# Where the weight buffers of a projection lie in the SBUF partition: moving them down, in a hybrid decoder block on one Trainium2 core

## The chip, the core and the metric

The kernel runs on one core of a Trainium2 chip. Its time is the device time of one execution, in microseconds; the time before is the median of three executions. Times inside the kernel come from one execution that the hardware profiler recorded.

## The reference, cut to what matters

All data is float32: 512 tokens, width 2048.

```python
h  = rms_norm(x, norm1_g);  z = h @ w_in                # 2048 -> 9216 columns in 72 tiles of 128
zs = token_shift(z[:, :3520], rw_mu)                    # r, k, v and three small inputs
o_rw  = rwkv7_mix(zs, ...)                              # 16 heads of 64, a recurrence over the tokens
o_att = swa_attention(q, k, v, ...)                     # 16 heads, window 128
p_rw, p_att = o_rw @ w_branch[:1024], o_att @ w_branch[1024:]
x = x + (sigmoid(zg_rw) * p_rw + sigmoid(zg_att) * p_att) @ w_out
x = x + conv_ffn(rms_norm(x, norm2_g), w_up, conv_w, conv_b, w_down)
```

## The kernel before

Every large product is made of float32r matmuls in threes: each operand is split into a high part (ACT, a copy) and a low part (DVE, a subtraction), and the products high·high, low·high and high·low are summed in PSUM. A matmul has a **stationary** operand (128 x 128, loaded by a LDWEIGHTS, engine PEld in the profile) and a **moving** one that streams past it.

The stages, in order of time:

- **Input projection with attention and RWKV inside it** (34.7 to 1240.3 us). `project` (L251) works on one tile of 128 columns: 16 steps over the width, each of three matmuls (L259 to L261) with 512 moving columns. Stationary are the weights `whi`, `wlo`; moving are the activations `xhi`, `xlo`. `load_w` (L237) brings weights in groups of four steps: SP issues the DMA into a buffer `raw` (L241), ACT writes `whi` (L244), DVE writes `wlo` (L245); every third group it also issues a step of the sums of the output weights (L228 on SP's queue, L229 on POOL's). There are 72 tiles, so 3456 such matmuls. The attention's and RWKV's small matmuls, which wait for ACT and DVE, stand between them; 32 gate tiles of the projection (`emit_gate`, L322) are kept back as filling, and the last of them stand behind RWKV. A scheduler orders the instructions; what is marked `pin` keeps the program's order.
- **Branch projection** (1240.3 to 1414.5 us): the same `project` and `load_w`, 768 matmuls; moving are `rhi`, `rlo` (RWKV's result) and `ahi`, `alo` (the attention's).
- **Output projection** (from 1414.5 us to about 1577): Strassen-like products in seven parts (`steps_of`, L944). Here the *left factors* `hhi`, `hlo` (from `fetch`, L937, which loads `hraw`) are stationary and the weights `whi`, `wlo` (pool hlD, L955 and L954) are moving, 512 columns (L962): 672 matmuls in threes with the stationary operands `hhi`, `hlo`, `hhi`.
- **Feed-forward up** (1577 to 2490 us): weights stationary, activations `b..`, `t..` moving with 256 columns (L1095). **Down** (2490 to 2914 us): `steps_of` again.

SBUF gives each of the 128 partitions one address range. Pools stand on it from two sides, "left" (growing up) and "right" (growing down). The places that the built programs give the operands of this study, in KiB from the start of the partition:

| operand | use | before | after the change |
|---|---|---|---|
| input projection `whi`, `wlo` | stationary | 204.0 to 216.0 (3 buffers each) | 97.8 to 113.8 (4 each) |
| its `raw` | DMA in | 216.0 to 224.0 | 89.8 to 97.8 |
| `xhi`, `xlo`; later `ahi`, `alo` | moving | 25.8 to 89.8 | the same |
| branch projection `whi`, `wlo` | stationary | 145.8 to 161.8 (4 each) | 97.8 to 113.8, the same buffers |
| `rhi`, `rlo` | moving | 89.8 to 121.8 | 113.8 to 145.8 |
| RWKV `BX`, `BV`, `BKK` | stationary | 105.9 to 117.9 | 129.9 to 141.9 |
| RWKV `AB`, `KK`, `SV`, `UV`, `AI`, `BT` | stationary | 125.9 to 129.9, 133.9 to 145.9, 147.9 to 155.9 | 141.9 to 165.9 |
| RWKV `BAR`, `MM` | moving | 117.9 to 125.9, 129.9 to 133.9 | 165.9 to 177.9 |
| RWKV `BKE` / `lg` (tag lw) / `lg`'s square / `gn` | stationary | 185 / 156 / 162 / 194 | 209 / 180 / 186 / 218 |
| attention `pr` | stationary | 157 to 165 | 181 to 189 |
| output projection `hhi` / `hlo` / `hraw` | stationary / stationary / DMA in | 178.7 to 184.7 / 184.7 to 190.7 / 172.7 to 178.7 | 172.7 to 178.7 / 178.7 to 184.7 / 184.7 to 190.7 |
| down `hhi`, `hlo` | stationary | 80.5 to 92.5 | 74.5 to 86.5 |
| weights of both Strassen stages and of up (`whi`, `wlo` of hlD) | moving / stationary in up | 18.5 to 42.5 | the same |
| `b11`, `b21`, `b22`, `t1`, `t3`, `t2`, `t4` | moving in up | 74.5 to 186.5 | the same |

## Time and profile before

| | |
|---|---|
| time, median of three executions | 2914.16 us (2914.02 to 2918.12) |
| span of the profiled execution, first to last instruction | 2913.7 us, 0.5 us below that median |
| PE busy | 98% of the span |
| chain that ended last | PE 94%, DVE 2%, ACT 1%, DMA 1% |
| granted TensorE clock | 0.997 over the span |

How to read it: a row of the costliest groups gives line, engine, operation, tiles (written<-read), shape and count, then busy time and the mean duration of one in ns. Matmuls are pipelined: a duration covers streaming and the way through the array, so one starts before the one ahead has ended, and durations of 390 ns stand for a start every 227 ns or so. The pace is therefore taken from counts in a stretch of time in which nothing but such matmuls run.

### The profile page before, as it was taken

Reading aid. Unit: us, or ns where it says so; the run is one execution under the profiler, and the core shown is the slowest. Engines: PE = TensorE matmul, PEld = TensorE weight load, DVE = VectorE, ACT = ScalarE, POOL = GpSimd, SP = SyncE. Lnnn points to the kernel's source line nnn. Section 1 sums busy time; section 2 is a strip of 40 time slices with the busy share of each in tenths; the row PEclk is TensorE's granted clock in tenths of the full one; section 3 lists DMA queues with packets and bytes.
Section 4 is the critical chain, followed back from the end, with each engine's and each line's share of the span. In section 5 each row is a group of like instructions: output and inputs, shape, how many; then the busy total and the mean of one; then the engine's idle time right before and its main releaser. Section 6 shows DMA issues by size and latency. Waiting matters only on the chain.

```text
span 2913.7 us, 46929 instructions
## 1 busy us (share of the span) xinstructions
PE 2868.1 (98%) x18014; PEld 2441.3 (84%) x18014; DVE 1970.2 (68%) x3383; ACT 1333.6 (46%) x2251; POOL 219.3 (8%) x286
## 2 busy tenths in 40 slices
PE   7999999999999999999999899999999999999999
PEld 5777777777777777788888899999999999888887
DVE  4577666667767766354567777787777777665565
ACT  4345435435435434322356455545555455544444
POOL 0001000000000000111000010111111100000000
PEclk9999999999999999999999999999999999999999
DMA  7856756656656655878877788988889888877775
GB/s 210 217 146 166 184 142 168 156 145 163 159 149 149 167 148 139 266 222 239 293 251 226 208 227 231 242 233 231 221 235 238 237 227 234 312 242 240 259 255 188
DMA packets 225137, 609.29 MB, mean 209 GB/s; under 512 B 24768, under 2 KB 44944, under 8 KB 223888
## 3 DMA queue, kind: packets, MB, share of 16 engines
q1 hardware_dynamic: 157504, 434.84, 45.9%
q0 software_dynamic: 36064, 132.14, 23.9%
q10 hardware_dynamic: 31344, 39.31, 4.0%
q8 instruction: 141, 2.31, 0.3%
q14 instruction: 84, 0.69, 0.1%
HBM read 556.54 MB, written 174.43 MB: 251 GB/s over the span
## 4 chain that ended last, share of the span: by engine, by line
PE 94%; DVE 2%; ACT 1%; DMA 1%; issue 0%; SPq 0%; DVEq 0%; ACTq 0%
PE X L1095 17%; PE acc L259 11%; PE X L962 11%; PE acc L261 11%; PE acc L260 11%; PE Y L1095 9%; PE Y L962 8%; PE Z L1095 4%; PE bulk L737 1%; PE bulk L690 1%; PE psG L744 1%; PE bulk L646 1%; PE psS L755 1%; PE mi L464 1%; PE scp L431 1%; PE bulk L554 1%
## 5 line engine op out<-in xcount | busy, mean ns | idle before, releaser
L259 PE MATMUL acc<-xhi,whi 128*128 128x512 f32 x1152 | 473.1, 411 | 5.0 <-ACT whi L244 3.1
L261 PE MATMUL acc<-xhi,wlo 128*128 128x512 f32 x1152 | 469.2, 408 | 0.0
L260 PE MATMUL acc<-xlo,whi 128*128 128x512 f32 x1152 | 467.1, 405 | 0.0
L244 ACT ACTIVATE whi<-raw 128x512 fp32r<-128x512 f32 x352 | 220.3, 630 | 492.8 <-PE acc L260 376.6
L955 DVE TENSOR_TENSOR wlo<-raw,whi 128x1024 fp32r<-128x1024 f32 x210 | 257.0, 1224 | 204.9 <-ACT whi L954 203.4
L245 DVE TENSOR_TENSOR wlo<-raw,whi 128x512 fp32r<-128x512 f32 x352 | 240.2, 689 | 207.3 <-ACT whi L244 195.4
L954 ACT ACTIVATE whi<-raw 128x1024 fp32r<-128x1024 f32 x210 | 222.8, 1061 | 287.9 <-PE X L962 147.1
L1095 PE MATMUL X<-b,whi 128*128 128x256 f32 x1472 | 270.2, 284 | 2.2 <-DVE u L1115 0.9
L1095 PE MATMUL X<-t,whi 128*128 128x256 f32 x1408 | 260.2, 285 | 8.7 <-DVE u L1115 8.3
L1078 DVE TENSOR_TENSOR wlo<-raw,whi 128x1024 fp32r<-128x1024 f32 x176 | 215.0, 1222 | 77.4 <-ACT whi L1077 77.2
L259 PEld LDWEIGHTS acc<-xhi,whi 128*128 128x128 f32 x1152 | 217.5, 189 | 52.8 <-ACT whi L244 4.4
L261 PEld LDWEIGHTS acc<-xhi,wlo 128*128 128x128 f32 x1152 | 217.3, 189 | 48.2 <-issue 2.2
L1095 PE MATMUL Y<-t,whi 128*128 128x256 f32 x1408 | 257.5, 283 | 0.0
L260 PEld LDWEIGHTS acc<-xlo,whi 128*128 128x128 f32 x1152 | 217.7, 189 | 44.9 <-issue 3.3
L1077 ACT ACTIVATE whi<-a 128x1024 fp32r<-128x1024 f32 x132 | 139.4, 1056 | 213.8 <-DVE a L1071 211.2
L1095 PEld LDWEIGHTS X<-b,whi 128*128 128x128 f32 x1472 | 230.3, 193 | 3.0 <-issue 2.3
L1095 PEld LDWEIGHTS X<-t,whi 128*128 128x128 f32 x1408 | 222.0, 194 | 9.3 <-DVE u L1115 5.7
L1095 PEld LDWEIGHTS Y<-t,whi 128*128 128x128 f32 x1408 | 220.1, 192 | 0.0
L1095 PE MATMUL X<-b,wlo 128*128 128x256 f32 x736 | 208.9, 284 | 2.1 <-DVE wlo L1078 2.1
L1078 DVE TENSOR_TENSOR wlo<-a,whi 128x1024 fp32r<-128x1024 f32 x132 | 161.7, 1225 | 67.7 <-ACT whi L1077 67.0
L1095 PE MATMUL X<-t,wlo 128*128 128x256 f32 x704 | 200.5, 285 | 0.0
L1095 PE MATMUL Y<-t,wlo 128*128 128x256 f32 x704 | 199.3, 283 | 0.0
(345 smaller groups left out, 5877.7 us busy)
## 6 DMA issues: line engine op xcount, KB each, us to landing
raw<-in_w_up_dram SPq DMA_DIRECT2D x180, 512.0 KB
raw<-in_w_z_dram SPq DMA_DIRECT2D x288, 256.0 KB
s_dn<-in_w_dn_dram POOLq DMA_DIRECT2D x88, 512.0 KB, 6.7
raw<-in_w_up_dram POOLq DMA_DIRECT2D x88, 512.0 KB, 8.1
raw<-s_dn SPq DMA_DIRECT2D x88, 512.0 KB
raw<-in_w_dn_dram SPq DMA_DIRECT2D x66, 512.0 KB
a<-in_w_up_dram SPq DMA_DIRECT2D x48, 512.0 KB
s_dn<-in_w_dn_dram SPq DMA_DIRECT2D x44, 512.0 KB
```

What stands on the lines that cost most here:

```text
L244: act.activation(hi, raw, AF.Copy)
L245: dve.tensor_tensor(lo, raw, hi.bitcast(F32), op=ALU.subtract)
L259: pe.matmul(acc, whi[:, j], xhi[:, k], start=first, stop=False)
L260: pe.matmul(acc, whi[:, j], xlo[:, k], start=False, stop=False)
L261: pe.matmul(acc, wlo[:, j], xhi[:, k], start=False, stop=last)
L431: pe.matmul(scp[e][:, j, k0:], qn[j][hs, ts], kd[g][hs, n * P - BLK + k0 : (n + 1) * P], start=True, stop=True)
L954: act.activation(whi, wr, AF.Copy)
L955: dve.tensor_tensor(wlo, wr, whi.bitcast(F32), op=ALU.subtract)
L962: pe.matmul(dst, l[:, q, ts], r[:, es], start=fst and j == 0, stop=lst and j == 2, skip_group_check=True)
L1077: pin(act.activation(hi, t, AF.Copy))
L1078: pin(dve.tensor_tensor(lo, t, hi.bitcast(F32), op=ALU.subtract))
L1095: pin(pe.matmul(ps, l[:, k], r[:, k], start=start and k + i == 0, stop=last and i == 2, skip_group_check=True))
```

## The change

The pool of the weight buffers is opened once, at the kernel's start, on the left side next to `xhi` and `xlo`, with four buffers each for `raw`, `whi` and `wlo`, and both projections use it; before, each projection opened its own (the input projection 4, 3 and 3 on the right, the branch projection 4, 4 and 4 on the left). RWKV's tiles are declared in another order, the left operands of its matmuls first, and `fetch` declares `hhi`, `hlo` before `hraw`. No arithmetic and no DMA is added or taken away.

```diff
     big1 = abc.enter_context(tc.tile_pool(name="big1", bufs=1))
+    wp = {"n": 0, "step": 3}
+    for nm in ("raw", "hl"):
+        wp[nm] = abc.enter_context(tc.tile_pool(name="w" + nm, bufs=4, reuse_waits="tile"))
     xin = ExitStack()
...
-    def open_weights(stack, nraw, nhl, side):
-        wp["raw"] = stack.enter_context(tc.tile_pool(name="wraw", bufs=nraw, side=side, reuse_waits="tile"))
-        wp["hl"] = stack.enter_context(tc.tile_pool(name="whl", bufs=nhl, side=side, reuse_waits="tile"))
...
-    open_weights(pa, 4, 3, "right")
...
+            AB, KK, SV, UV = (bd.tile([P, NCH, 2, C], F32, name=n) for n in ("AB", "KK", "SV", "UV"))
+            AI = bd.tile([P, 2, NCH, P], F16, name="AI")
+            BT = bd.tile([P, 2, NCH, P], F16, name="BT")
...
             BAR = bd.tile([P, NCH, 2, 2, C], F32, name="BAR")
...
-            AB, MM, KK, SV, UV = (bd.tile([P, NCH, 2, C], F32, name=n) for n in ("AB", "MM", "KK", "SV", "UV"))
...
+            MM = bd.tile([P, NCH, 2, C], F32, name="MM")
             Et = bd.tile([P, NCH, C + 1], F32, name="Et")
             pool.memset(Et[:, :, 0:1], 1.0)
-            AI = bd.tile([P, 2, NCH, P], F16, name="AI")
-            BT = bd.tile([P, 2, NCH, P], F16, name="BT")
...
-        open_weights(pbb, 4, 4, "left")
...
+        hhi, hlo = (pl.tile([P, 2, TH], F32R, name=f"h{e}", tag=f"h{e}") for e in ("hi", "lo"))
         hr = pl.tile([P, 2, TH], F32, name="hraw", tag="hraw")
         pin(sync.dma_start(hr, right_d[w][c][RIGHT_AT[PRODUCTS[i][3]]]))
-        hhi, hlo = (pl.tile([P, 2, TH], F32R, name=f"h{e}", tag=f"h{e}") for e in ("hi", "lo"))
```

In the order of the built programs, PE's instructions from RWKV to the end stand as before; inside the attention some matmuls change places by a few positions, and the two score matmuls of the first block of a head group (L431) stand up to 56 projection matmuls later. On ACT and DVE a few of the splits L244 and L245 stand one place earlier or later. On SP's queue the loads of the branch projection's first weights, eight of which stood among the last loads of the input projection, now follow all of these, and the gate loads of the first tile (L891) stand before the last 17 loads of the input projection.

More of the change, by code (lines that the diff above doesn't have):

```diff
@@ L229, in sums_along @@
         return lambda: pool.dma_start(dst, quarter(w, second, c)[q], accum_op=ALU.add, max_dma_last_dim=4096)
-    wp = {"n": 0, "step": 3}
-    def open_weights(stack, nraw, nhl, side):
-        wp["raw"] = stack.enter_context(tc.tile_pool(name="wraw", bufs=nraw, side=side, reuse_waits="tile"))
-        wp["hl"] = stack.enter_context(tc.tile_pool(name="whl", bufs=nhl, side=side, reuse_waits="tile"))
     def load_w(src):
@@ L529, in block_kernel @@
             BKK = bd.tile([P, NCH, P], F32, name="BKK")
+            AB, KK, SV, UV = (bd.tile([P, NCH, 2, C], F32, name=n) for n in ("AB", "KK", "SV", "UV"))
+            AI = bd.tile([P, 2, NCH, P], F16, name="AI")
+            BT = bd.tile([P, 2, NCH, P], F16, name="BT")
+            pool.memset(SV[0:C, 0, 0], 0.0)
+            pool.memset(SV[C:P, 0, 1], 0.0)
             BAR = bd.tile([P, NCH, 2, 2, C], F32, name="BAR")
@@ L532, in block_kernel @@
             pool.memset(BAR[C:P, :, 0], 0.0)
-            AB, MM, KK, SV, UV = (bd.tile([P, NCH, 2, C], F32, name=n) for n in ("AB", "MM", "KK", "SV", "UV"))
-            pool.memset(SV[0:C, 0, 0], 0.0)
-            pool.memset(SV[C:P, 0, 1], 0.0)
+            MM = bd.tile([P, NCH, 2, C], F32, name="MM")
             Et = bd.tile([P, NCH, C + 1], F32, name="Et")
             pool.memset(Et[:, :, 0:1], 1.0)
-            AI = bd.tile([P, 2, NCH, P], F16, name="AI")
-            BT = bd.tile([P, 2, NCH, P], F16, name="BT")
             def r3(ap, c=C):
```

## The prediction

> **What bounds the kernel now.** I read the page first, then the waits of PE in the input projection, then one question the page can't answer: how fast a full-size matmul follows the next, stage by stage.

> ```profile
> PE 2868.1 (98%) x18014; PEld 2441.3 (84%) x18014; DVE 1970.2 (68%) x3383; ACT 1333.6 (46%) x2251; POOL 219.3 (8%) x286
> ...
> PE 94%; DVE 2%; ACT 1%; DMA 1%; issue 0%; SPq 0%; DVEq 0%; ACTq 0%
> ...
> L259 PE MATMUL acc<-xhi,whi 128*128 128x512 f32 x1152 | 473.1, 411 | 5.0 <-ACT whi L244 3.1
> L261 PE MATMUL acc<-xhi,wlo 128*128 128x512 f32 x1152 | 469.2, 408 | 0.0
> L260 PE MATMUL acc<-xlo,whi 128*128 128x512 f32 x1152 | 467.1, 405 | 0.0
> ```

> PE sets the end nearly everywhere, and in the input projection (3 x 1152 = 3456 matmuls of 512 columns) it hardly waits: 5.0 us before L259, none before L260 and L261. So only what shortens PE's own steps, or its few waits, counts.

> The next view is the table by stage, for stretches in which nothing but such matmuls run: two of the input projection (272 and 1220 us), the branch projection, the output projection, the down projection. Columns: stretch, length, busy time and count of each engine, granted clock, DMA share, GB/s.

> ```profile
> 272.00:314.00 42.00, 42.00 (x182) 34.09 (x181) 17.00 (x27) 14.26 (x23) 8.36 (x15) 1.00 0.79 215
> 1220.00:1239.00 19.00, 19.00 (x83) 15.43 (x82) 5.87 (x9) 5.67 (x10) 1.63 (x2) 1.00 0.89 242
> 1245.00:1405.00 160.00, 160.00 (x707) 132.54 (x706) 79.61 (x134) 40.34 (x66) 17.01 (x24) 1.00 0.83 253
> 1416.00:1555.00 139.00, 139.00 (x597) 111.84 (x596) 90.86 (x110) 72.34 (x98) 7.99 (x14) 1.00 0.78 259
> 2500.00:2900.00 400.00, 400.00 (x1767) 331.31 (x1766) 238.10 (x245) 193.95 (x220) 0.00 (x0) 1.00 0.76 255
> ```

> Length by count (halfway between the counts of PE and PEld, as pieces at the edges are counted too): 42.0/181.5 = 231.4 ns, 160/706.5 = 226.5, 139/596.5 = 233.0, 400/1766.5 = 226.4. The clock is 1.00 in all of them. The groups by line inside the same stretches say it in durations:

> ```profile
> L260 PE MATMUL acc<-xlo,whi 128*128 128x512 f32 x61 | 24.1, 395 | 0.0
> L259 PE MATMUL acc<-xhi,whi 128*128 128x512 f32 x61 | 24.1, 394 | 0.0
> L261 PE MATMUL acc<-xhi,wlo 128*128 128x512 f32 x60 | 23.7, 395 | 0.0
> ```
> ```profile
> L259 PE MATMUL acc<-ahi,whi 128*128 128x512 f32 x128 | 49.8, 389 | 0.0
> ```
> ```profile
> L962 PE MATMUL Y<-whi,hhi 128*128 128x512 f32 x96 | 38.3, 399 | 0.0
> L962 PE MATMUL Y<-wlo,hhi 128*128 128x512 f32 x96 | 37.8, 394 | 0.0
> L962 PE MATMUL Y<-whi,hlo 128*128 128x512 f32 x96 | 37.6, 392 | 0.0
> ```
> ```profile
> L962 PE MATMUL Y<-whi,hhi 128*128 128x512 f32 x264 | 102.7, 389 | 0.0
> ```

> Input projection 394.7 on average, branch 389; output 395, down 389. The pairs are what matters. Input and branch projection are the same three lines, with the same moving addresses (`ahi` lies where `xhi` lay); output and down are the same line with the same moving addresses. In each pair the one thing that differs and explains the pace is where the stationary operand lies: at 204 to 216 KiB and at 178.7 to 190.7 KiB it is slow, at 145.8 to 161.8 KiB and at 80.5 to 92.5 KiB fast. ACT, DVE and DMA are about as busy in the slow stretches as in the fast ones. So I read: a weight load from above some line between 161.8 and 178.7 KiB costs a 512-column matmul 5 to 7 ns.

> **The change part by part.** *1. The input projection's weights go from 204 to 216 KiB to 97.8 to 113.8 KiB.* That is below the line. Gain 394.7 - 389 = 5.7 ns x 3456 = **19.7 us**. By the counts the bounds are 231.4 - 226.5 = 4.9 ns (16.9 us) and, if the whole step of the output pair holds, 233.0 - 226.4 = 6.6 ns (22.8 us). I take 5.7, the stage's own row.

> *2. What the gain meets.* In RWKV's stretch the fast matmuls are filling between links that wait for ACT and DVE; there a shorter filling only lengthens a wait.

> ```profile
> 350.00:1166.00 816.00, 814.21 (x5412) 614.16 (x5411) 545.96 (x1317) 353.69 (x793) 52.47 (x66) 1.00 0.61 153
> ```
> ```profile
> 350.00:1166.00 816.00, 303.41 (x731) 137.72 (x731) 1.00 0.61 153
> ```
> ```profile
> PEld psS L755 <- ACT UV L749: 15.4, 42, 0.4
> PEld psG L744 <- DVE SV L757: 12.7, 36, 0.8
> ...
> PEld bulk L737 <- ACT BX L728: 6.5, 27, 0.3
> ```

> The first row is the whole stretch, the second L259 alone, which runs 731 times, so 3 x 731 = 2193 of the 3456 matmuls stand there. If all their gain were eaten, 2193 x 5.7 = 12.5 us would go. But weight loads come late at only 42 + 36 + 27 = 105 links, and PE itself is busy for 814.21 of the 816 us; I let each such link eat the gain of four matmuls (my choice for a short run): 105 x 4 x 5.7 ns = **2.4 us lost** (0 to 12.5).

> *3. Four `whi`, `wlo` buffers in place of three, and SP's order.* ACT can split one group further ahead. Eight early loads of branch weights leave the tail of the input projection, where a `raw` that lands late already stops PE:

> ```profile
> PE acc L259 <- ACT whi L244: 3.1, 3, 1.6
> ```
> ```profile
> ACT whi L244 <- DMA raw<-in_w_z_dram: 21.5, 6, 7.6
> ```
> ```profile
> 1155.98 6.48 SPq L241 DMA_DIRECT2D raw<-in_w_z_dram  x2
> 1164.26 2.61 SPq L241 DMA_DIRECT2D raw<-in_w_b_dram  x3
> 1166.98 0.38 SPq L241 DMA_DIRECT2D raw<-in_w_z_dram  x1
> ```

> Between 0 and 3.1 us comes back; I take **1.5 us**. Behind it on SP's queue: the gate load L891 now stands ahead of 17 loads of `raw` and waits for PE's last reads of `KK`, whose place it takes. Before, SP stood there too, for the branch loads (issued only at 1164.26). Four buffers of 12 matmuls cover 4 x 12 x 227 ns = 10.9 us of such a stop, so I cost it at nothing; a stop longer than that would fall on PE in full. The branch projection begins without its own prefilled buffers, but runs on the ring that has fed the stage before it: also nothing, bounded by the 3.1 us that late loads cost in the tail.

> *4. RWKV and attention operands move up by 24.5 KiB.* `AB` to `BT`, stationary, end at 165.9 KiB: 4 KiB above the highest place that I know to be fast. Those that cross the line are float32: `pr` (112 loads), `lg` and its square (64 each). Float32 loads show no rise with place: `BKE` at 185 against `BX` at 106 KiB, and `gn` at 194 against `sqq` at 124.

> ```profile
> L662 PE MATMUL bulk<-ident,BX 128*128 128x128 f32 x64 | 10.0, 279 | 0.1
> L674 PE MATMUL bulk<-ident,BKE 128*128 128x128 f32 x64 | 10.1, 280 | 0.2
> L334 PE MATMUL mi<-cst,sqq 128*128 128x2 f32 x80 | 10.1, 248 | 0.0
> L334 PE MATMUL bulk<-cst,gn 128*128 128x2 f32 x64 | 7.8, 243 | 0.0
> ```

> Nor do moving operands: `b` at 74 to 122 KiB and `t` at 122 to 186 KiB stream alike, so `BAR` and `MM` may go up.

> ```profile
> L1095 PE MATMUL X<-b,whi 128*128 128x256 f32 x1472 | 270.2, 284 | 2.2 <-DVE u L1115 0.9
> L1095 PE MATMUL X<-t,whi 128*128 128x256 f32 x1408 | 260.2, 285 | 8.7 <-DVE u L1115 8.3
> ```

> Zero; at most (112 + 64 + 64) x 6.6 ns = 1.6 us lost.

> *5. `hhi`, `hlo` go down by 6 KiB.* `hlo` comes to lie exactly where `hhi` was slow; `hhi` lies between 172.7 and 178.7, in the unknown gap but close to its slow end. Gain 0, at most two loads of three: 2/3 x 672 x 6.6 ns = 3.0 us. In the down stage all places stay low: nothing.

> **Sum:** 19.7 - 2.4 + 1.5 = 18.8 us off the profiled execution, 2913.7 - 18.8 = 2894.9 us; the median stands 0.5 us above that execution, so **2895.4 us**. A measurement here tells apart about 0.2%, or 5.8 us.

> **The rivals.**

> *The links eat it (2906).* For: the 105 late loads, and two thirds of the matmuls stand among links. Against: PE stands still for under 2 us there. Price: all 12.5 us in place of 2.4 lost, and nothing back in the tail: 2914.2 - 19.7 + 12.5 = 2907.0; with the tail's 1.5 us 2905.5. I say 2906.

> *The place of the weights is not the cause (2914).* The slow stages would be slow for another reason, such as the links of RWKV beside them. Then only part 3 is left: 2914.2 - 1.5 + 1 = about 2914. Against: the output projection has no RWKV beside it, and the step at 1240 us comes with the new pool. [...]

> *Nearness costs (2937).* Weights would then lie within 8 KiB of `xlo` and right below `rhi`. If what slows a load is not its height but that PE reads both operands from one region, the new place pays at each matmul: 6.6 ns x 3456 = 22.8 us, 2937. It turns from gain to loss if nearness costs more than the 5.7 ns that height gives back. For: no row shows a distance under 32 KiB. Against: at 32 to 38 KiB (down stage, weights up to 42.5, factors from 80.5) the pace is the fast one.

> **How the numbers follow.** Forecast 0.74, links 0.12, no cause 0.07, nearness 0.07. Around the forecast: best 22.8 + 3.1 + 3.0 = 28.9 us (2885.3), worst the links' 2907.0. The range 2886 to 2907 takes in the first two cases, less their edges; about 0.16 is left out. Faster by over 0.2%: 0.74 + 0.12 = 0.86; within: 0.07; slower: 0.07.

> **What would show it.** Right: L259 to L261 on `xhi`, `xlo` at 389 ns in stretches without links, and 48 of them per 10.9 us; L259 from RWKV's stretch below 415 ns; the output projection still at 392 to 399. Part 5 is wrong if those fall; part 2 if the waits at L755, L744, L737 grow well beyond 34.6 us in all; part 3 if PE waits for `whi` by more than before around 1165 to 1245 us. The whole is wrong if L259 to L261 stay at 394 or 395.

## The result, and the profile after

| | before | after |
|---|---|---|
| time, median of five executions | 2917.22 us (2914.02 to 2918.30) | 2902.51 us (2901.29 to 2908.26) |
| ratio, 95% interval | | 0.9961 (0.9949 to 0.9974) |
| span of the profiled execution | 2913.7 us | 2900.2 us |
| its granted TensorE clock | 0.997 | 0.998 |

The forecast was 2895.4 us (2886 to 2907), that is 18.8 us less than before; measured are 14.7 us by the medians and 13.5 us by the spans. The interval of the ratio stands for 7.6 to 14.9 us, so the forecast gain is too large by a quarter at least. The sign was right, and the time lies inside the forecast's range. The cause that the forecast gave was wrong, as the experiments show.

From here on lines are those of the kernel after: `project` has its three matmuls at L256 to L258, `load_w` its splits at L241 and L242, `steps_of` its matmul at L958. First the page of the kernel after: busy time of each engine, the chain that ended last, and the costliest groups.

```profile
PE 2854.5 (98%) x18014; PEld 2436.3 (84%) x18014; DVE 1969.8 (68%) x3383; ACT 1333.8 (46%) x2251; POOL 219.1 (8%) x286
...
PE 93%; DVE 2%; ACT 2%; DMA 1%; issue 1%; ACTq 0%; POOL 0%; SPq 0%; DVEq 0%; POOLq 0%
...
L256 PE MATMUL acc<-xhi,whi 128*128 128x512 f32 x1152 | 467.9, 406 | 1.9 <-DVE xlo L303 1.9
L258 PE MATMUL acc<-xhi,wlo 128*128 128x512 f32 x1152 | 464.5, 403 | 0.0
L257 PE MATMUL acc<-xlo,whi 128*128 128x512 f32 x1152 | 463.2, 402 | 0.0
```

The counts are the same to the last instruction, and PE still sets the end. Each of the three lines is 3 to 5 ns shorter on average than before, and the waits ahead of them fell from 5.0 to 1.9 us. The same groups in a stretch of the input projection without links, 268 to 310 us:

```profile
L258 PE MATMUL acc<-xhi,wlo 128*128 128x512 f32 x63 | 24.5, 389 | 0.0
L256 PE MATMUL acc<-xhi,whi 128*128 128x512 f32 x62 | 24.1, 389 | 0.0
L257 PE MATMUL acc<-xlo,whi 128*128 128x512 f32 x62 | 24.1, 389 | 0.0
```

389 ns, as in the branch projection. From the start of one matmul to the start of the next (worked out from the single records) this stretch takes 226.7 ns, the one of before 232.4: 5.7 ns, the step that the forecast used. (The forecast's 231.4 came from counts in a window; a matmul lasts 390 ns, so a window counts one that began before it, and counts make the pace some 0.4% too fast in 42 us. The differences hardly change.)

The table by stage of the kernel after, for the whole of RWKV's stretch, the tail of the input projection, the branch, the output and the down projection (columns as in the prediction):

```profile
343.00:1158.50 815.50, 813.58 (x5439) 617.01 (x5438) 549.60 (x1327) 358.10 (x802) 52.93 (x67) 1.00 0.62 154
```
```profile
1161.00:1226.70 65.70, 65.48 (x287) 53.28 (x287) 24.34 (x47) 20.34 (x35) 10.59 (x16) 1.00 0.89 271
```
```profile
1250.00:1390.00 140.00, 139.62 (x615) 115.09 (x615) 64.76 (x111) 33.12 (x54) 15.51 (x21) 1.00 0.83 250
1404.00:1542.00 138.00, 138.00 (x593) 111.03 (x592) 89.83 (x108) 72.30 (x98) 7.52 (x14) 1.00 0.79 260
2500.00:2880.00 380.00, 380.00 (x1678) 314.65 (x1677) 228.27 (x236) 185.96 (x212) 0.00 (x0) 1.00 0.77 253
```

And the tail of the kernel before, over the same instructions:

```profile
1168.50:1240.50 72.00, 68.72 (x288) 53.07 (x288) 24.85 (x49) 20.91 (x36) 10.56 (x16) 1.00 0.86 263
```

Where the 13.5 us came from, by the starts of the same instructions in both traces:

| stage | before, us | after, us | difference |
|---|---|---|---|
| input projection up to the first `lg` statistic | 280.1 | 276.1 | -4.0 |
| from there to the last `gn` statistic (RWKV) | 853.8 | 850.3 | -3.5 |
| from there to the first matmul of the branch projection (tail) | 71.9 | 65.7 | -6.2 |
| branch projection | 174.1 | 174.9 | +0.8 |
| output, up, down | 160.4, 913.8, 419.8 | 160.2, 913.4, 419.8 | -0.6 |

The tail holds only 1/12 of the matmuls and gave nearly half. RWKV holds two thirds of them and gave a quarter. Eight later kernels are the same as the kernel after up to RWKV's end. Their RWKV row is between 850.5 and 853.4 us, and most of that spread has a reason of its own: in the six with 851.6 us or more the granted clock was 0.50 for 3.41 us, from 340 to 342 us on, for which I estimate up to 1.7 us, half of that time. The two without it have 850.5 and 851.0, and the two traces of the table have none in this stretch. So RWKV's share is about 3 us (2.8 to 3.5). The branch projection took 174.1 us in all eight, as before, so the 0.8 us belongs to this one execution.

### The profile page after: what moved, and what is told of

Same layout as the page of the kernel before. It is cut to its first block, busy times and chain, and to the rows that moved or that the text cites. A ratio compares the mean times of both kernels' runs of the same rounds, so it can differ in the third digit from the quotient of the medians.

```text
span 2900.2 us, 46951 instructions
## 1 busy us (share of the span) xinstructions
PE 2854.5 (98%) x18014; PEld 2436.3 (84%) x18014; DVE 1969.8 (68%) x3383; ACT 1333.8 (46%) x2251; POOL 219.1 (8%) x286
## 3 DMA queue, kind: packets, MB, share of 16 engines
q0 software_dynamic: 36064, 132.14, 24.1%
## 4 chain that ended last, share of the span: by engine, by line
PE 93%; DVE 2%; ACT 2%; DMA 1%; issue 1%; ACTq 0%; POOL 0%; SPq 0%; DVEq 0%; POOLq 0%
PE X L1091 17%; PE X L958 11%; PE acc L256 11%; PE acc L258 11%; PE acc L257 11%; PE Y L958 9%; PE Y L1091 8%; PE Z L1091 4%; PE bulk L734 1%; PE bulk L687 1%; PE bulk L643 1%; PE psG L741 1%; PE psS L752 1%; PE mi L460 1%; PE bulk L551 1%
## 5 line engine op out<-in xcount | busy, mean ns | idle before, releaser
L256 PE MATMUL acc<-xhi,whi 128*128 128x512 f32 x1152 | 467.9, 406 | 1.9 <-DVE xlo L303 1.9
L258 PE MATMUL acc<-xhi,wlo 128*128 128x512 f32 x1152 | 464.5, 403 | 0.0
L241 ACT ACTIVATE whi<-raw 128x512 fp32r<-128x512 f32 x352 | 221.1, 630 | 490.0 <-PE acc L257 400.0
L242 DVE TENSOR_TENSOR wlo<-raw,whi 128x512 fp32r<-128x512 f32 x352 | 240.7, 689 | 205.3 <-ACT whi L241 193.4
L1074 DVE TENSOR_TENSOR wlo<-raw,whi 128x1024 fp32r<-128x1024 f32 x176 | 214.9, 1222 | 77.8 <-ACT whi L1073 77.7
L258 PEld LDWEIGHTS acc<-xhi,wlo 128*128 128x128 f32 x1152 | 216.6, 188 | 44.7 <-issue 3.2
L256 PEld LDWEIGHTS acc<-xhi,whi 128*128 128x128 f32 x1152 | 216.6, 188 | 44.6 <-DVE xlo L303 2.1
L1091 PEld LDWEIGHTS X<-b,whi 128*128 128x128 f32 x1472 | 230.7, 193 | 3.1 <-issue 2.4
```

The source lines that it names most:

```text
L241: act.activation(hi, raw, AF.Copy)
L242: dve.tensor_tensor(lo, raw, hi.bitcast(F32), op=ALU.subtract)
L256: pe.matmul(acc, whi[:, j], xhi[:, k], start=first, stop=False)
L258: pe.matmul(acc, wlo[:, j], xhi[:, k], start=False, stop=last)
L1074: pin(dve.tensor_tensor(lo, t, hi.bitcast(F32), op=ALU.subtract))
L1091: pin(pe.matmul(ps, l[:, k], r[:, k], start=start and k + i == 0, stop=last and i == 2, skip_group_check=True))
```

## The experiments

All ratios are to the kernel before. A kernel without an interval was executed once, and its trace is what counts.

**Buffers or place?** First the number of buffers by itself: four of each in the old place.

```diff
-    open_weights(pa, 4, 3, "right")
+    open_weights(pa, 4, 4, "right")
```

> The kernel before with four whi, wlo buffers in place of three, still at the partition's upper end (200 to 216 KiB), nothing else changed. Theory (the place of the weights sets the pace): full-size matmuls of the input projection stay at 231.4 ns in stretches without links; only the late splits of the tail may go, about 4 us at most, so a ratio of 0.9985 to 1.0. Rival (the fourth buffer and the order it allows brought the 13.7 us): about the time of the kernel after, ratio 0.995 to 0.997.

Measured: 2914.67 us, ratio 0.9996 (0.9987 to 1.0005). The stretch of full-size matmuls, by stage, and PE's waits in its tail:

```profile
272.00:314.00 42.00, 42.00 (x182) 34.08 (x181) 16.49 (x27) 14.26 (x23) 8.35 (x15) 1.00 0.85 231
```
```profile
PE acc L259 <- ACT whi L244: 0.8, 1, 0.8
```

182 in 42 us, as before (232.4 ns). The tail took 69.0 in place of 71.9 us and its wait for `whi` fell from 3.1 to 0.8 us. So in this trace a fourth buffer is worth 2.9 us of the tail's 6.2, and nothing of the pace; the whole time shows no gain that is clear of noise. Then three buffers in the new place:

```diff
-        wp[nm] = abc.enter_context(tc.tile_pool(name="w" + nm, bufs=4, reuse_waits="tile"))
+        wp[nm] = abc.enter_context(tc.tile_pool(name="w" + nm, bufs=4 if nm == "raw" else 3, reuse_waits="tile"))
```

> The kernel after with three whi, wlo buffers in place of four, still in the lower half (97.8 to 109.8 KiB). Theory (place): 226.7 ns in long runs and nearly the whole gain, ratio 0.996 to 0.9975. Rival (fourth buffer): the gain falls to a third or less, ratio 0.9985 to 1.0, with 231 ns.

Measured: 2906.68 us, ratio 0.9971 (0.9961 to 0.9981); 226.7 ns, and a tail of 65.9 us without late splits: the gain in pace does not need the fourth buffer, and in the shared ring the tail doesn't either. But the branch projection took 180.5 in place of 174.1 us. PE's waits there:

```profile
PE acc L258 <- DVE wlo L242: 2.1, 2, 1.4
PE acc L256 <- ACT whi L241: 1.1, 1, 1.1
PE acc L256 <- ACT rhi L210: 0.5, 1, 0.5
```

Here the three buffers run dry at the change of stage, where ACT and DVE split `rhi` and `ahi` as well. In the kernel after the only such wait is 0.4 us.

**The order of RWKV's tiles.** The change puts the left operands first; this kernel takes back that part alone (the declarations of the kernel before).

```diff
-            AB, KK, SV, UV = (bd.tile([P, NCH, 2, C], F32, name=n) for n in ("AB", "KK", "SV", "UV"))
-            AI = bd.tile([P, 2, NCH, P], F16, name="AI")
-            BT = bd.tile([P, 2, NCH, P], F16, name="BT")
...
             BAR = bd.tile([P, NCH, 2, 2, C], F32, name="BAR")
...
-            MM = bd.tile([P, NCH, 2, C], F32, name="MM")
+            AB, MM, KK, SV, UV = (bd.tile([P, NCH, 2, C], F32, name=n) for n in ("AB", "MM", "KK", "SV", "UV"))
...
+            AI = bd.tile([P, 2, NCH, P], F16, name="AI")
+            BT = bd.tile([P, 2, NCH, P], F16, name="BT")
```

> The kernel after with RWKV's tiles declared in the order of the kernel before: SV, UV, AI and BT, left operands of some 1600 to 1900 small matmuls, then lie at 161.9 to 179.9 KiB in place of 149.9 to 165.9. Theory (only matmuls with 512 moving columns lose by a high left operand): the time of the kernel after, ratio 0.9961 within 0.0007. Rival (every weight load from up there costs its matmul 6.6 ns): 1600 x 6.6 ns = 10.6 us more, ratio about 0.9997.

Measured: 2906.01 us, ratio 0.9966 (0.9954 to 0.9979). The interval overlaps that of the kernel after (0.9949 to 0.9974), and the rival's 0.9997 lies outside it. RWKV took 853.1 us; this execution too had a granted clock of 0.50 for 3.41 us from 341 us on, and with this order the scheduler also sets some small matmuls otherwise. This part of the change does nothing that can be measured.

**Is it the height?** The forecast says that loads from above a line near 162 to 179 KiB are slow. The next two kernels were to find that line: one puts the output projection's factors 8 KiB lower, by swapping them with the buffers `tq`, the other puts the down projection's factors at 161 to 173 KiB.

```diff
     hps = ExitStack()
+    mp = hps.enter_context(tc.tile_pool(name="mt", bufs=2, side="right", reuse_waits="tile"))
     hp = hps.enter_context(tc.tile_pool(name="hhlC", bufs=3, side="right", reuse_waits="tile"))
...
-        mp = pbb.enter_context(tc.tile_pool(name="mt", bufs=2, side="right", reuse_waits="tile"))
```

> The kernel after with the output projection's factors 8 KiB lower (hhi at 164.7 to 170.7, hlo at 170.7 to 176.7 KiB, the buffers tq above them). Theory (place, a line somewhere between 161.8 and 172.7 KiB): two thirds of the 672 matmuls read hhi; if the line lies above 170.7 the stage loses 2/3 x 672 x 6.7 = 3.0 us, if it lies in the middle of hhi half of that, if it lies below 164.7 nothing; from 161.5 us to between 158.5 and 161.5. Beside it each buffer lies in 2 KiB of its own, so the steps of the single buffers show the line. Rival (something else than place slows this stage): 161.5 us and 233 ns whatever the buffer.

```diff
+                    pad = pd.enter_context(tc.tile_pool(name="pad", bufs=1, reuse_waits="tile"))
+                    pad.tile([P, 22144], F32, name="pad")
                     hp0 = pd.enter_context(tc.tile_pool(name="hhl", bufs=3, reuse_waits="tile"))
```

> The kernel after with hhi at 161 to 167 and hlo at 167 to 173 KiB in the down stage (an unused tile of 86.5 KiB lies below them): one weight load reads 0.5 KiB of each partition, so the steps show at which address the pace turns from 226.5 to 233 ns. Theory (a line): one address between 161.8 and 172.7, fast below it and slow above. Rival (the cost grows evenly with the address): a slope over the whole of the 12 KiB.

The output projection with its factors at 164.7 to 176.7 KiB (first row; 2903.86 us, ratio 0.9957, 0.9945 to 0.9970), and the down projection with its factors at 161 to 173 KiB (second; 2903.8 us, one execution):

```profile
1404.00:1542.00 138.00, 138.00 (x593) 111.01 (x593) 90.05 (x111) 72.68 (x99) 7.25 (x13) 1.00 0.78 258
```
```profile
2700.00:2860.00 160.00, 160.00 (x708) 132.48 (x707) 96.22 (x100) 77.66 (x89) 0.00 (x0) 1.00 0.78 262
```

The first is as slow as at 172.7 to 184.7 (593 in 138 us; 233.3 ns), from its lowest buffer on. The second is fast throughout (226.7 ns). Both have their moving operands at 18.5 to 42.5 KiB. The same heights are slow in one stage and fast in the other, so **there is no line**, and the forecast's cause falls.

Three more kernels move the down projection's operands to the upper end: the stationary ones, the moving ones, both.

```diff
-                    hp0 = pd.enter_context(tc.tile_pool(name="hhl", bufs=3, reuse_waits="tile"))
+                    hp0 = pd.enter_context(tc.tile_pool(name="hhl", bufs=3, side="right", reuse_waits="tile"))
```

> The kernel after with the factors hhi, hlo (stationary) of the down stage at the upper end (206 to 218 KiB) from its second step on; everything else, the moving weights at 18.5 to 42.5 KiB too, as it was. Theory (stationary place): 1824 matmuls at 233 in place of 226.5 ns, 1824 x 6.5 = 12 us slower than the kernel after, about 2914 and a ratio near 1.0. Rival (place is not the cause): the time of the kernel after, ratio 0.996, 226.5 ns.

```diff
+                    hlp = pd.enter_context(tc.tile_pool(name="hlE", bufs=3, side="right", reuse_waits="tile"))
...
-                steps_of("dn", i, acc[nm], c, hp0, first_h if i == 0 and c == 0 else None)
+                steps_of("dn", i, acc[nm], c, hp0, first_h if i == 0 and c == 0 else None, hlp)
```

> The kernel after with the moving operands of the down stage (whi, wlo) at the upper end (200 to 224 KiB) from its second step on, and the stationary ones low (74.5 to 86.5). Theory (only the stationary operand's place counts): ratio 0.996 as in the kernel after, 226.5 ns. Rival (the moving operand's place counts for 512 columns as well): up to 12 us slower than the kernel after, ratio near 1.0.

> The kernel after with stationary (206 to 218 KiB) and moving operands (182 to 206 KiB) of the down stage both high. If only the stationary place counts: 233 ns, about 2914 us. If both count and add: 239 ns or more, about 2926 us. If what counts is that the two lie far apart: 226.5 ns, about 2902 us.

Measured: stationary high 2932.27 us, ratio 1.0059 (1.0044 to 1.0074); moving high 2934.07 us, 1.0066 (1.0049 to 1.0083); both high 2915.57 us, one execution. In this order, the same 160 us of the stage:

```profile
2700.00:2860.00 160.00, 160.00 (x687) 128.54 (x686) 91.72 (x94) 75.46 (x86) 0.00 (x0) 1.00 0.75 249
```
```profile
2700.00:2860.00 160.00, 160.00 (x687) 128.81 (x686) 91.32 (x94) 75.39 (x87) 0.00 (x0) 1.00 0.76 249
```
```profile
2700.00:2860.00 160.00, 160.00 (x707) 132.48 (x707) 96.63 (x100) 77.17 (x89) 0.00 (x0) 1.00 0.78 260
```

233.3, 233.3 and 226.7 ns. Moving either operand costs the same 6.6 ns, moving both costs nothing: what counts is a relation of the two. (The times also hold a side effect of these kernels: the new place comes free late, and PE stands once at the stage's start, here of the first and the third kernel:

```profile
PE X L958 <- ACT hhi L210: 13.7, 1, 13.7
```
```profile
PE X L958 <- ACT hhi L210: 11.6, 1, 11.6
```

The stage took 447.6 and 432.9 us against 419.8. Less these waits 14.1 and 1.5 us are left. The 1.5 of the third, which has no loss of pace, is what follows the stop, where the granted clock stayed at 0.50 for about 4 us (of 13.65 in all); and 14.1 - 1.5 = 12.6 us is the pace, where 1824 x 6.6 makes 12.0.)

**The relation.** Two readings fit "both high is fast": that the operands must not be far apart, or that their addresses must agree modulo some number of bytes. The second fits `dn_line` too, where they are 119 to 155 KiB apart and fast. So I wrote down the exact addresses of every pair modulo 512, where the front part of this document had rounded them to a tenth of a KiB:

| stage and kernel | stationary | moving | difference mod 256 | ns from start to start |
|---|---|---|---|---|
| input projection, before | 480 | 352 | 128 | 232.4 |
| input projection, after | 352 | 352 | 0 | 226.7 |
| branch projection, both | 352 | 352 | 0 | 226 to 227 |
| output projection, both | 160 | 0 | 160 | 233.3 |
| the same 8 KiB lower | 160 | 0 | 160 | 233.3 |
| down, before, after, and at 161 to 173 KiB | 0 | 0 | 0 | 226.7 |
| down, stationary high | 480 | 0 | 224 | 233.3 |
| down, moving high | 0 | 480 | 32 | 233.3 |
| down, both high | 480 | 480 | 0 | 226.7 |

Pools on the left grow from one address, pools on the right shrink from another, and the two differ by a remainder. Every fast pair of this table has both operands in pools of one side, every slow pair one on each. The four kernels that follow test this theory, each with the remainder alone.

The old place, with 128 bytes in between so that the remainders agree:

```diff
     def open_weights(stack, nraw, nhl, side):
+        if side == "right":
+            stack.enter_context(tc.tile_pool(name="pad", bufs=1, side=side)).tile([P, 32], F32, name="pad")
         wp["raw"] = stack.enter_context(tc.tile_pool(name="wraw", bufs=nraw, side=side, reuse_waits="tile"))
```

> The kernel before with an unused tile of 128 bytes between raw and the weights of the input projection: whi, wlo stay at the upper end (203.8 to 215.8 KiB) but now stand at the same remainder modulo 512 bytes as xhi, xlo (352 and 352; before 480 and 352). New theory (what slows a 512-column matmul is that stationary and moving operand differ modulo 512 bytes): pace from 231.4 to about 227 ns, 7 to 11 us gained without any move to the lower half, ratio 0.9965 to 0.9980 (the late loads of the tail stay). Forecast's theory (a high place is slow): 231.4 ns, ratio 0.9995 to 1.0005.

Measured: 2909.25 us, ratio 0.9978 (0.9969 to 0.9987). The stretch without links, and PE's waits in the tail:

```profile
268.00:310.00 42.00, 42.00 (x187) 34.79 (x186) 17.11 (x27) 14.66 (x25) 8.35 (x15) 1.00 0.82 223
```
```profile
PE acc L261 <- ACT whi L246: 3.0, 1, 3.0
```

187 in 42 us and 226.7 ns, at the upper end of the partition. The first part took 275.8 us and RWKV 850.6, as in the kernel after. Only the tail kept its late loads (70.9 us; right behind the stop of 3.0 us the granted clock was 0.50 for 3.41 us, for which I estimate some 1.6 us, a little under half of that time). This is the whole gain in pace without the move; the rest of the change's gain is the tail's.

The same in the output projection, which the change had left slow:

```diff
     hps = ExitStack()
+    hps.enter_context(tc.tile_pool(name="padC", bufs=1, side="right")).tile([P, 40], F32, name="padC")
```

> The kernel after with an unused tile of 160 bytes above the output projection's factors, so hhi, hlo lie 160 bytes lower, still at 172.5 to 184.5 KiB, and at the remainder of whi, wlo modulo 512 bytes (0 and 0; after 160 and 0). New theory (remainder): pace of the output projection from 233.0 to 226.6 ns, 672 x 6.4 = 4.3 us less than the kernel after, ratio about 0.9946, and faster than both kernels. Forecast's theory (a high place is slow): 233 ns, ratio 0.9961.

Measured: 2901.23 us, ratio 0.9950 (0.9937 to 0.9962). Its table by stage, and its groups by line (`steps_of` stands at L959 there), beside the same groups of the kernel after:

```profile
1404.00:1542.00 138.00, 138.00 (x611) 114.21 (x610) 93.18 (x116) 73.42 (x99) 8.00 (x14) 1.00 0.80 268
```
```profile
L959 PE MATMUL Y<-whi,hhi 128*128 128x512 f32 x96 | 37.3, 389 | 0.0
L959 PE MATMUL Y<-whi,hlo 128*128 128x512 f32 x96 | 37.3, 389 | 0.0
L959 PE MATMUL Y<-wlo,hhi 128*128 128x512 f32 x96 | 37.3, 389 | 0.0
```
```profile
L958 PE MATMUL Y<-whi,hhi 128*128 128x512 f32 x96 | 38.3, 399 | 0.0
L958 PE MATMUL Y<-wlo,hhi 128*128 128x512 f32 x96 | 37.8, 394 | 0.0
L958 PE MATMUL Y<-whi,hlo 128*128 128x512 f32 x96 | 37.6, 392 | 0.0
```

160 unused bytes, and the stage falls from 160.2 to 156.1 us (4.1; expected 4.3). The times of this kernel and of the kernel after differ by 1.3 us at the median and their intervals overlap; that the stage is faster stands on the trace. Its median is the lowest of the fourteen kernels of this study.

Which remainders count? The down projection with a shift that changes every 130 or so matmuls:

```diff
+    SHIFT = (((0, 0), (32, 32)), ((4, 4), (16, 16)), ((64, 64), (128, 128)), ((160, 160), (256, 256)), ((320, 320), (384, 384)), ((448, 448), (480, 480)), ((0, 160), (160, 0)))
...
+        if w == "dn" and (i or c):
+            offs = SHIFT[i][c > 5]
+            hhi, hlo = (pl.tile([P, 2 * TH + P], F32R, name=f"h{e}", tag=f"h{e}")[:, o // 4 : o // 4 + 2 * TH]
+                        .rearrange("p (q s) -> p q s", q=2) for e, o in zip(("hi", "lo"), offs))
```

> The kernel after with the down stage's factors hhi, hlo still low (74.5 to 89.5 KiB) but shifted by a number of bytes that changes from block to block of some 130 matmuls: 0, 32, 4, 16, 64, 128, 160, 256, 320, 384, 448, 480, then only hlo by 160, only hhi by 160. New theory (remainder modulo 512): 226.6 ns at 0 and 231 to 238 ns at the others, some 8 to 12 us in all; which of the small shifts and whether 256 counts is open, and tells the modulus. Forecast's theory (height): 226.6 ns at all of them and the time of the kernel after.

Measured: 2913.59 us, one execution; the stage took 429.1 us, 9.3 more than in the kernel after. From start to start, inside each block:

| shift, bytes | 0 | 4 | 16 | 32 | 64 | 128 | 160 | 256 | 320 | 384 | 448 | 480 | `hlo` 160 | `hhi` 160 |
|---|---|---|---|---|---|---|---|---|---|---|---|---|---|---|
| ns | 226.7 | 232.4 | 233.3 | 233.3 | 233.3 | 232.4 | 233.4 | 226.7 | 233.3 | 232.3 | 228.9 | 233.3 | 233.3 | 231.1 |

Three blocks in the table by stage: shifts of 0, of 32 and of 256 bytes.

```profile
2490.00:2510.00 20.00, 20.00 (x90) 16.53 (x90) 11.10 (x12) 10.46 (x12) 0.00 (x0) 1.00 1.03 409
2513.00:2537.00 24.00, 24.00 (x104) 19.35 (x103) 13.47 (x14) 11.05 (x13) 0.00 (x0) 1.00 0.74 240
...
2698.00:2722.00 24.00, 24.00 (x107) 19.89 (x106) 13.70 (x16) 11.63 (x13) 0.00 (x0) 1.00 0.74 234
```

107 against 104 in 24 us: 256 bytes are as good as none, four bytes cost 5.7 ns. So the period is 256 bytes, not 512. Shifts of 128 and of 384, equal modulo 256, agree at 232.4 and 232.3 ns; that is also the input projection of before (128). Only 448 (192) lies in between, which the theory doesn't say. And it isn't enough that one of the two factors agrees: with only `hlo` shifted, which one matmul in three loads, the mean is 233.3 ns, as with both shifted (233.4).

**Where RWKV's share went.** In the kernel after, sorted by their place in a run of full-size matmuls, the steps from start to start in RWKV's stretch (before and after, ns; from the single records) are:

| place in the run | count | before | after | sum of the difference, us |
|---|---|---|---|---|
| first, to the second | 325 | 330.9 | 330.8 | 0.0 |
| 2nd to 4th | 523 | 232.3 | 230.7 | -0.8 |
| 5th to 10th | 506 | 232.4 | 228.4 | -2.1 |
| 11th on | 551 | 232.5 | 226.7 | -3.3 |
| last, to a small matmul | 394 | 312.2 | 320.8 | +3.4 |
| between small ones, and to the first | 3290 | 77.8 | 77.6 | -0.7 |

Three quarters of the steps that start from a full-size matmul are too near a small one to have the whole 5.7 ns. The 719 first and last steps gain nothing, the 1029 in places 2 to 10 half of it, 2.9 us in all, and only the 551 from the 11th on have all of it. Of the 6.2 us that are gained, 3.4 are lost again in the steps from the last full-size matmul to a small one. This 3.4 is uncertain: the last row holds 123.0 us before and 124.6 in `ring4_high`, whose pace is the same, and between 125.1 and 126.7 in the kernels with the faster pace, so the loss is between 0.5 and 3.7 us. It is not found at the three links of the forecast; PEld's waits there are what they were (15.4, 12.7 and 6.5 us before):

```profile
PEld psS L752 <- ACT UV L746: 15.3, 42, 0.4
PEld psG L741 <- DVE SV L754: 12.8, 36, 0.8
...
PEld bulk L734 <- ACT BX L725: 6.8, 27, 0.3
```

Is the loss of pace near a small matmul real, without any link? In the down projection nothing waits. There a small matmul after each 12 full-size ones, with a shift in every second product, separates the two losses. (Its left operand is zero, so it adds nothing to the sums. The shift is made as in the last kernel. The trace holds two records of each: 41 of them in 60 us without the shift, between 241 full-size matmuls, or 20 runs of 12.)

```diff
+            if zero is not None and not lst:
+                pe.matmul(acc[0][0][:, :P], zero, ident, start=False, stop=False, skip_group_check=True)
```

> The kernel after with one small float32 matmul (left operand all zeros, so it adds nothing) after each 12 full-size matmuls of the down stage, and hhi, hlo shifted by 160 bytes in every second product. Theory on where the gain went in RWKV's stretch (a run of full-size matmuls gets the faster pace only after some ten of them): between the small matmuls positions 1 to 3 take 230 to 231 ns with and without the shift, the later ones differ by 1 to 6 ns, so shifted and unshifted products differ by 25 to 35 ns for a run of 12 in place of 12 x 6.4 = 77 ns. Rival (the gain is lost in waits for ACT and DVE alone): the whole 60 to 77 ns for a run.

Measured: 2949.26 us, one execution. A product without shift, then one with 160 bytes:

```profile
2616.00:2676.00 60.00, 60.00 (x282) 49.64 (x282) 30.89 (x31) 26.54 (x31) 0.00 (x0) 1.00 0.69 220
2682.00:2742.00 60.00, 60.00 (x279) 49.09 (x278) 30.54 (x31) 25.86 (x31) 0.00 (x0) 1.00 0.68 219
```

From the second record of one small matmul to the first of the next, by the single records: 2885 ns without and 2918 with the shift. So a run of 12 gains 33 ns where 12 x 6.6 = 79 would be the whole; per matmul 2.8 in place of 6.6 ns. The expected 25 to 35 ns held, the rival's 60 to 77 did not. But it held for the sum alone. Of the 33 ns, 12 fall on the steps at the small matmul, where the expectation had nothing; behind them the single places alternate between 224 and 236 ns without the shift and between 231 and 238 with it, in a fixed pattern, and not in the order that was expected. So in this run a small matmul nearby costs more than half of the gain (46 of 79 ns) even where nothing waits; that the pace recovers step by step is shown for RWKV's stretch only.

## Why the prediction was right, and where it was wrong

```profile
L261 PE MATMUL acc<-xhi,wlo 128*128 128x512 f32 x23 | 9.4, 408 | 0.0
L260 PE MATMUL acc<-xlo,whi 128*128 128x512 f32 x23 | 9.1, 395 | 0.0
L259 PE MATMUL acc<-xhi,whi 128*128 128x512 f32 x22 | 9.0, 409 | 3.1 <-ACT whi L244 3.1
```

The fourth buffer alone is worth 2.9 us of it; the shared ring with three buffers, in `low_ring3`, all of it. No run separates the ring from the order of SP's loads that comes with it. The gate load ahead of SP's last loads cost nothing that PE's waits show. The start of the branch projection cost nothing either (174.1 us in eight of nine traces); with three buffers it costs 6.4.
- **4, RWKV's operands.** Zero was right: `old_order` is the same within its interval. But the rows quoted could not have shown a rise. For "Nor do moving operands" they were matmuls of 256 columns whose operands agree modulo 256 bytes in every case, `b` and `t` alike; `BX` and `BKE` both differ from `ident` by 32 bytes. For 512 columns the moving operand counts as much as the stationary one (233.3 ns in `dn_mov_high` and in `dn_stat_high`).
- **5, the output factors.** Zero was right (160.4 and 160.2 us), by luck, as the reason was wrong: not that 172.7 lies above a line, but that 160 bytes stay 160 bytes when a pool slides by 6 KiB.
- **The rivals.** "The place of the weights is not the cause" was right in its name and wrong in its price: the move changed the remainder with the place, so the gain came all the same. (The 1 us added in its price stands on no row.) In the runs the paces 226.7 and 233.3 ns of the same matmuls depend on both addresses together (`dn_stat_high`, `dn_mov_high`, `dn_both_high`). "Nearness costs" is excluded: weights 8 KiB from `xlo` run at 226.7 ns. Its "no row shows a distance under 32 KiB" was a slip: in the branch projection of before, `rlo` ended 24 KiB below the weights, at the fast pace. "The links eat it" was nearest in RWKV's stretch, where most of the gain was lost, though not at the links; the tail gave more than it allowed.

By the stages of the table, the 18.8 us of the forecast were 5.0 up to RWKV (878 matmuls), 10.7 in RWKV (2299 matmuls, less 2.4) and 3.1 in the tail (279, and 1.5); measured were 4.0, 3.5 and 6.2, and -0.2 elsewhere, 13.5 in all. So an error of 7 us in RWKV and one of 3 us the other way in the tail partly cancel, which is luck. The range held because the pair of stages gave the price of the effect correctly, whatever its cause.

What stays open: why 192 bytes modulo 256 (shift 448) costs only a third (2.2 of 6.6 ns); whether the load or the stream is held up (the recorded durations of the weight loads are 188 ns in both kernels' stretches); why a run in RWKV's stretch needs some ten matmuls to reach the faster pace; and whether 256-column matmuls lose as well, since all of those in the up stage agree and no run shifted them.

## What to carry to other kernels

Before a stage of back-to-back 512-column float32r matmuls is tuned, write down the exact byte addresses of its stationary and its moving operand modulo 256: in this kernel an unused tile of 160 bytes that made them agree took 4.1 us off the output projection (160.2 to 156.1), and 2.8% off its pace (233.3 to 226.7 ns). Pools on different sides of the partition differed here by a remainder that no one had chosen: 32, 128, 160 or 224 bytes modulo 256. And when two stages differ in pace, a table of rounded addresses hides one candidate; vary one property by itself (the same place shifted by 128 bytes) before naming another.

## What the hardware did unexpectedly

- In the down projection of `dn_shift` a 512-column float32r matmul started every 226.7 ns where stationary and moving operand agree modulo 256 bytes (shifts of 0 and 256), every 232.3 to 233.4 ns at differences of 4, 16, 32, 64, 128, 160 and 224 bytes, and every 228.9 at 192 (shift 448). The granted clock was 1.00 in all of these stretches.
- Behind the small matmuls of RWKV's stretch the faster pace came only by and by in the kernel after: 230.7 ns in places 2 to 4, 228.4 in 5 to 10, 226.7 from the 11th on, where the disagreeing pair of before shows 232.3 to 232.5 at all of them.
- With PE's stops of 11.6 and 13.7 us at the start of the down projection the granted clock was 0.50 for 13.65 us: it fell 2.7 and 4.1 us after the last matmul ahead of the stop had started, and was back at 1.00 about 4 us after PE went on. With the stop of 3.0 us in the tail of `high_aligned` it was 0.50 for 3.41 us, right behind the stop. Over 30 us the mean is 0.77, where the kernel after, without the stop, has 1.00 (first the kernel with the stationary operands high, then the kernel after):

```profile
2475.00:2505.00 30.00, 15.68 (x68) 12.24 (x69) 14.88 (x21) 9.05 (x12) 0.00 (x0) 0.77 0.85 321
```
```profile
2475.00:2505.00 30.00, 29.34 (x131) 23.90 (x130) 21.38 (x27) 15.94 (x20) 2.13 (x4) 1.00 0.96 373
```
